# The feed-forward of a transformer block with its weights as the stationary operand of each matmul

## The chip, the cores and the metric

One core of a Trainium2 chip runs the whole program. The metric is the device time of one execution in microseconds; of the kernel before, three runs took 2580.87, 2583.21 and 2591.02 us. One core has a matmul engine (TensorE, PE in the profile, with a lane of its own for weight loads, PEld), VectorE (DVE), ScalarE (ACT), GpSimd (POOL) and SyncE (SP); POOL and SP here mostly issue transfers (DMA).

## What is computed

One layer on 512 tokens of width 2048, all in float32: an input projection, a state-space branch and a differential attention branch, their merge, an output projection, and a gated feed-forward network. Only the last part changes:

```python
x = x + m @ w_out[l]
h = rms_norm(x, norm2_w[l], RMS_EPS)
x = x + (jax.nn.silu(h @ w_ffn_gate[l]) * (h @ w_ffn_up[l])) @ w_ffn_down[l]
```

`rms_norm` divides each token by the root of its mean square and multiplies by a weight per column. The feed-forward width is 5632. The output is x, and the program hands it over transposed, as 2048 columns of the model by 512 tokens (`out` is (D, T); the host turns it round after the run, as it did before).

## The kernel before

**Numbers.** Every large product splits both operands into a high part (float32r, `hi`) and the rest (`lo`), and adds three matmuls: high by high, high by low, low by high. For weights ScalarE copies `raw` into `whi`, and VectorE subtracts into `wlo` (`split`, lines 529 and 530).

**Seven products instead of eight.** The feed-forward cuts each product of matrices into 2 x 2 blocks and computes seven block products (a Winograd form), numbered 1 to 7 in the code. For gate and up, the blocks of x are halves of the tokens (256 each) by halves of the model width (1024 each), and the blocks of the weights are halves of the width by gate and up. For down, they are halves of the tokens by halves of the inner width, and the two column halves of a 1024-column part of `w_ffn_down`. Sums of x blocks are formed once per operand; sums of weight blocks are formed on VectorE as they stream in, in the slab `A` and in `raw` buffers, or by an adding transfer of POOL's queue (line 1316).

**Staging.** The inner width of 5632 is cut into 11 units of 512. For each unit, `ffn` calls `seven` (line 1043) with n = 8 blocks of 128 along the width: each of the seven products is streamed in four chunks of weights, a chunk being 256 rows by 512 columns. `seven` asks `weights(i, c)` for the chunk, splits it, issues its matmuls, and after the last chunk of product i calls `done(i, banks)`, which empties the accumulators into the pieces of the result. Between chunks it pops closures from `fill`. The products of a unit run in the order 1, 2, 7, 5, (6, 3), 4, where (6, 3) means that the chunks of 6 and 3 alternate. Products 6, 3 and 4 go on accumulating in the banks of 1, 5 and 7.

After the 11 units, down runs in six blocks of units ([0], [1, 2], ..., [9, 10]), each for two halves v of the model's columns: 22 unit-halves of seven products with one chunk per unit. Results accumulate in SBUF under the names "11", "5", "7", "x", "53" and "74", after the products in them, and the last block combines them.

**Form A.** A matmul holds a 128 x 128 stationary operand and streams the other one through. Here the stationary one is a tile of 128 tokens (`xh`, `xl`), and the moving one 512 columns of weights: a chunk has 2 blocks x 2 token tiles x 3 = 12 matmuls of 128x512. The results lie with tokens on the partitions. The next stage wants them the other way round, so `flips` (line 1217) transposes 128x128 pieces through TensorE into PSUM banks T and O; in the units, `flip_act` copies them back on ScalarE (line 1254), and `make` forms the seven operands for down from them, which go to memory (`opd`, line 1270) and come back in the down blocks. At the end `final` transposes the finished blocks, adds the residual x2, which lies in memory, and stores.

**Roots.** The reciprocal root of a token's mean square is a value per token. With tokens on the partitions it is a column of scalars (`self.r2`), which ScalarE takes as the scale of its SiLU (line 1333 and 1351) and VectorE as the scalar of a fused multiply (lines 1347 and 1352).

**Order.** TensorE's order is the program's (`manual_schedule`). On the other engines a planner orders the instructions by priority; within an engine they run in the order planned. PSUM has eight banks: four `lin`, two `S`, `T`, `O`. In form A products 1 and 7 take `lin`, 2 and 5 take `S`, the transposes `T` and `O`.

## Time and profile before

| | us |
|---|---|
| median of three runs | 2583.21 |
| the profiled execution | 2578.66 |
| its span, first to last instruction | 2576.9 |
| TensorE busy | 2515.5 |
| VectorE busy | 1912.4 |
| ScalarE busy | 1149.3 |
| first matmul of the feed-forward | 1248 |
| last matmul of the feed-forward ends | 2568.7 |

A row of the groups reads: line, engine, operation, output<-inputs, shapes, count | busy us, mean ns of one | idle time of the engine just ahead of it and what ended it. The time of a matmul in a row is from its start to its end; the next starts before that end, so the pace is read from starts. A chronological row reads: start us, us, engine, line, operation, output<-inputs, shapes, count of like instructions merged. A row of stretches gives busy time and count of each engine in a stretch, the TensorE clock that was granted (1.00 is full), the share of the transfer engines, and GB/s.

### The profile page before, as it was taken

The numbers are of one execution on the slowest core, as the hardware profiler recorded it, in microseconds if no ns is written. First come the engines' busy times: TensorE is split into PE (matmuls) and PEld (weight loads), VectorE is DVE, ScalarE is ACT, GpSimd is POOL, SyncE is SP. The second block draws the span as 40 slices with busy tenths as digits, with TensorE's granted clock in tenths as the row PEclk, the third lists the DMA queues.
The fourth block names the chain that finished last, engine by engine and source line by source line (L and its number), as shares of the span: only waits on it lengthen the run. The fifth ranks groups of instructions, "written<-read, shape, count | busy, mean of one in ns | idle before, by whom it ended". The sixth has DMA issues, their size and how long they took to land.

```text
span 2576.9 us, 32218 instructions
## 1 busy us (share of the span) xinstructions
PE 2515.5 (98%) x11655; PEld 2051.2 (80%) x11655; DVE 1912.4 (74%) x3024; ACT 1149.3 (45%) x1544; POOL 317.4 (12%) x491
## 2 busy tenths in 40 slices
PE   8999999999999999999999999999999998999999
PEld 7788888777777778888788787888888887888887
DVE  7876664777678875535778787788877787788788
ACT  4123332654455543224555554555555555333332
POOL 1012221100010110000001111111101111000000
PEclk9999999999999999999999999999999999999999
DMA  6544554866753434433667666667667697667774
GB/s 190 159 131 124 143 145 132 301 223 221 243 196 104 142 111 156 157 110 129 229 165 219 203 197 208 200 205 236 188 201 208 200 289 289 208 208 236 247 230 150
DMA packets 256400, 491.85 MB, mean 191 GB/s; under 512 B 43448, under 2 KB 43768, under 8 KB 256240
## 3 DMA queue, kind: packets, MB, share of 16 engines
q1 hardware_dynamic: 194160, 352.50, 41.9%
q0 software_dynamic: 49504, 133.04, 18.6%
q10 hardware_dynamic: 12576, 4.24, 0.8%
q8 instruction: 92, 1.51, 0.2%
q14 instruction: 68, 0.56, 0.1%
HBM read 420.35 MB, written 71.96 MB: 191 GB/s over the span
## 4 chain that ended last, share of the span: by engine, by line
PE 50%; issue 30%; DMA 7%; DVE 7%; POOL 4%; ACT 1%; ACTq 0%; SPq 0%; POOLq 0%; DVEq 0%
PE lin L521 24%; PE lin L1068 12%; PE S L1068 8%; DMA raw<-in_w_in_dram 3%; DVE wlo L530 3%; POOL opd L1270 2%; POOL s L1316 1%; DVE raw L1082 1%; DMA raw<-in_w_ffn_up_dram 1%; DVE s L1232 1%; PE S L714 1%; ACT whi L529 1%; DMA s<-in_w_ffn_up_dram 1%; PE S L472 1%; PE O L744 1%
## 5 line engine op out<-in xcount | busy, mean ns | idle before, releaser
L1068 PE MATMUL lin<-whi,s 128*128 128x512 f32 x2400 | 767.4, 393 | 3.3 <-DVE wk L839 2.4
L521 PE MATMUL lin<-s,whi 128*128 128x512 f32 x2432 | 747.6, 397 | 12.5 <-ACT s L535 7.1
L529 ACT ACTIVATE whi<-s 128x1024 fp32r<-128x1024 f32 x351 | 371.0, 1060 | 426.5 <-PE lin L1068 198.8
L521 PEld LDWEIGHTS lin<-s,whi 128*128 128x128 f32 x2432 | 452.8, 189 | 121.5 <-issue 14.1
L1068 PE MATMUL S<-whi,s 128*128 128x512 f32 x1680 | 544.0, 392 | 2.9 <-DVE wk L1232 2.0
L1068 PEld LDWEIGHTS lin<-whi,s 128*128 128x128 f32 x2400 | 453.9, 189 | 99.1 <-issue 2.7
L530 DVE TENSOR_TENSOR wlo<-s,whi 128x1024 fp32r<-128x1024 f32 x351 | 427.7, 1222 | 132.0 <-ACT whi L529 127.6
L1068 PE MATMUL lin<-wlo,s 128*128 128x512 f32 x1200 | 473.2, 394 | 19.9 <-DVE wlo L530 19.9
L521 PE MATMUL lin<-s,wlo 128*128 128x512 f32 x1216 | 455.1, 393 | 0.0
L1068 PEld LDWEIGHTS S<-whi,s 128*128 128x128 f32 x1680 | 315.4, 188 | 68.3 <-ACT whi L529 3.7
L500 DVE TENSOR_TENSOR wlo<-raw,whi 128x1024 fp32r<-128x1024 f32 (+1 forms) x153 | 185.9, 1215 | 218.3 <-ACT whi L499 211.7
L1068 PE MATMUL S<-wlo,s 128*128 128x512 f32 x840 | 328.0, 391 | 6.5 <-DVE wlo L530 6.5
L499 ACT ACTIVATE whi<-raw 128x1024 fp32r<-128x1024 f32 (+1 forms) x153 | 161.0, 1053 | 364.0 <-PE lin L521 324.2
L529 ACT ACTIVATE whi<-raw 128x1024 fp32r<-128x1024 f32 x190 | 199.6, 1057 | 234.5 <-DVE raw L1082 88.0
L1068 PEld LDWEIGHTS lin<-wlo,s 128*128 128x128 f32 x1200 | 227.1, 189 | 77.6 <-DVE wlo L530 31.4
L530 DVE TENSOR_TENSOR wlo<-raw,whi 128x1024 fp32r<-128x1024 f32 x190 | 230.2, 1221 | 56.1 <-ACT whi L529 55.6
L521 PEld LDWEIGHTS lin<-s,wlo 128*128 128x128 f32 x1216 | 229.4, 189 | 48.4
L1068 PEld LDWEIGHTS S<-wlo,s 128*128 128x128 f32 x840 | 157.8, 188 | 42.2 <-DVE wlo L530 10.5
L1270 POOL DMA_DIRECT2D opd<-wk x154 | 90.2, 593 | 679.0 <-ACT wk L529 610.8
L1232 DVE TENSOR_TENSOR s<-s,raw 128x1024 f32<-128x1024 f32 x79 | 96.4, 1222 | 8.9 <-DMA raw<-in_w_ffn_up_dram 7.1
L1082 DVE TENSOR_TENSOR raw<-raw,raw 128x1024 f32<-128x1024 f32 x48 | 58.6, 1224 | 35.4 <-DMA raw<-in_w_in_dram 34.6
L530 DVE TENSOR_TENSOR wk<-s,wk 128x512 fp32r<-128x512 f32 x77 | 52.8, 686 | 39.8 <-DMA opd<-wk 32.2
(409 smaller groups left out, 2330.9 us busy)
## 6 DMA issues: line engine op xcount, KB each, us to landing
raw<-in_w_in_dram SPq DMA_DIRECT2D x175, 512.0 KB, 4.3
raw<-in_w_ffn_up_dram SPq DMA_DIRECT2D x83, 512.0 KB, 4.6
opd<-wk POOLq DMA_DIRECT2D x154, 256.0 KB, 3.8
s<-opd SPq DMA_DIRECT2D x77, 512.0 KB, 9.2
s<-in_w_ffn_down_dram SPq DMA_DIRECT2D x65, 512.0 KB, 6.4
s<-in_w_ffn_gate_dram SPq DMA_DIRECT2D x60, 512.0 KB, 5.1
s<-in_w_ffn_up_dram SPq DMA_DIRECT2D x48, 512.0 KB, 4.2
s<-in_w_ffn_gate_dram POOLq DMA_DIRECT2D x44, 512.0 KB, 7.5
```

The lines of the kernel that those rows point to most:

```text
L472: state = lambda ri, **kw: nc.tensor.matmul(y[:, q * P:(q + 1) * P], w2[:, ri, q].rearrange("p k c -> p (k c)"), sd[:, ri, q].rearrange("p ...
L499: nc.scalar.activation(hi[:, ks], raw[:, ks], AF.Copy)
L500: nc.vector.tensor_tensor(lo[:, ks], raw[:, ks], hi[:, ks].bitcast(F32), op=ALU.subtract)
L521: nc.tensor.matmul(acc[b], l, r, start=(k == 0 and i == 0), stop=(k == nk - 1 and i == 2))
L529: ins = self.nc.scalar.activation(hi, x, AF.Copy)
L530: self.nc.vector.tensor_tensor(lo, x, hi.bitcast(F32), op=ALU.subtract)
L714: nc.tensor.matmul(sp[m], qT[ms, h, i * P:(i + 1) * P], kT[ms, h, 0:W], start=True, stop=True)
L744: nc.tensor.matmul(op[:, h * P:(h + 1) * P], pT[:, kt * P:(kt + 1) * P], v[:, kt, (4 * half + h) * P:(4 * half + h + 1) * P], start=(kt == ...
L1068: nc.tensor.matmul(banks[i][tt], l, r[:, kk, :], skip_group_check=True, start=(i in own and k == 0 and q == 0), stop=(k == n - 1 and q == 2))
L1082: add = lambda o, x, y, op=ALU.add: tt(o, x, y, op=op)
L1232: add = lambda eng, o, x, y, op=ALU.add: eng.tensor_tensor(o, x, y, op=op)
L1270: pool.dma_start(opd[u, i - 1, :, h], hl[h].bitcast(F32))
```

## The change

`seven` gets a `form` argument. In form B, which both feed-forward stages now use, a 128 x 128 tile of weights is stationary and 256 tokens are moving: a chunk has 4 column tiles x 2 blocks x 3 = 24 matmuls of 128x256, two column tiles sharing a bank. The results lie with inner or model columns on the partitions, as the next stage and the output want them. `flips`, `flip_act` and their copies are gone.

A token is now a column, so the roots are needed as a row: `row` multiplies the identity by the scalars and sums it with ones on TensorE, once (`R2`). VectorE multiplies the gate by this row ahead of the SiLU (`silu`), and the finished blocks at the end; the scalar of the fused multiplies is gone. SiLU and its products are put into a list `later`, from which a closure is run ahead of a later chunk's weights.

In the units the order becomes 1, (2, 7), 5, (6, 3), 4, and product 5 takes the banks T and O. In down, "5" and "7" become one accumulator "57"; in the last block some sums of weights are made by adding transfers. `final` multiplies by the row, has x2 added by a transfer (POOL's queue) and stores, up to two stores behind; one piece ("74" of the last half) is finished in `done` of the last product.

On TensorE, at the first chunk of product 2 of a unit in the middle of gate and up. Names: S, O and lin are PSUM banks, whi and wlo the parts of a chunk's weights, s the operand slabs of x, fw and row the results to be transposed; a number tells one buffer from another, and x2 stands for two like instructions in a row. Before, the end of that chunk, four transposes, and the next chunk of product 2:

```order
L1068 MATMUL S_12430<-whi_12433,s_1730_10245 128x512
L1068 MATMUL S_12430<-wlo_12434,s_1730_10245 128x512
L1068 MATMUL S_12430<-whi_12433,s_1730_10245 128x512
L1222 MATMUL O_12449<-ident,fw_12275 128x128
L1222 MATMUL O_12449<-ident,fw_12278 128x128
L1222 MATMUL O_12449<-ident,row_12091 128x128
L1222 MATMUL O_12449<-ident,fw_12094 128x128
L1068 MATMUL S_12429<-whi_12457,s_1730_10245 128x512
L1068 MATMUL S_12429<-wlo_12458,s_1730_10245 128x512
```

Now the end of that chunk, and the first chunk of product 7 behind it:

```order
L1075 MATMUL S_15295<-s_1730_10245,whi_15299 128x256 x2
L1075 MATMUL S_15295<-s_1730_10245,wlo_15300 128x256
L1075 MATMUL S_15295<-s_1730_10245,whi_15299 128x256 x2
L1075 MATMUL S_15295<-s_1730_10245,wlo_15300 128x256
L1075 MATMUL lin_15296<-s_1694_9962,whi_15332 128x256 x2
L1075 MATMUL lin_15296<-s_1694_9962,wlo_15333 128x256
L1075 MATMUL lin_15296<-s_1694_9962,whi_15332 128x256 x2
L1075 MATMUL lin_15296<-s_1694_9962,wlo_15333 128x256
```

The transposes no longer stand between the chunks, the matmuls are half as wide and twice as many, and the chunks of 2 and 7 take turns.

On VectorE, at the end of a unit: lin is the end of product 4, which the two operations with lin add up; wlo_13601 and, now, wlo_15234 are the splits of the third chunk of the next unit's product 1. Before:

```order
L1232 TENSOR_TENSOR c_2247_13461<-c_2247_13461,lin_13133 128x512
L1232 TENSOR_TENSOR s_2248_13464<-s_2248_13464,lin_13134 128x512
L530 TENSOR_TENSOR wlo_13601<-s_1814_10830,whi_13600 128x1024
L1352 SCALAR_TENSOR_TENSOR row_13298<-row_13298,rs_10624,c_2247_13461 128x512
L1352 SCALAR_TENSOR_TENSOR fw_13301<-fw_13301,rs_10624,s_2248_13464 128x512
L530 TENSOR_TENSOR wlo_13618<-s_1814_10830,whi_13617 128x1024
L530 TENSOR_TENSOR wlo_13641<-s_1847_11045,whi_13640 128x1024
L530 TENSOR_TENSOR wlo_13664<-s_1847_11045,whi_13663 128x1024
```

Now:

```order
L1239 TENSOR_TENSOR c_2229_15010<-c_2229_15010,lin_14378 128x512
L1239 TENSOR_TENSOR s_1814_10972<-s_1814_10972,raw_15390 128x1024
L1239 TENSOR_TENSOR s_2230_15013<-s_2230_15013,lin_14379 128x512
L1239 TENSOR_TENSOR c_2229_15010<-c_2229_15010,row_11142 128x512
L530 TENSOR_TENSOR wlo_15234<-s_1814_10972,whi_15233 128x1024
L1239 TENSOR_TENSOR s_2230_15013<-s_2230_15013,row_11142 128x512
L530 TENSOR_TENSOR wlo_15263<-s_1814_10972,whi_15262 128x1024
L1239 TENSOR_TENSOR fw_14763<-fw_14763,c_2229_15010 128x512
L1239 TENSOR_TENSOR fw_14766<-fw_14766,s_2230_15013 128x512
L530 TENSOR_TENSOR wlo_15300<-s_1853_11338,whi_15299 128x1024
```

Ahead of that split stood the two additions; now they have a sum of weights (raw_15390) between them and a multiply by the row (row_11142) behind, and the products with fw, plain now, stand two splits after the additions.

The diff, cut to what matters:

```diff
-    def seven(self, n, weights, ops, done, order=ORDER, fill=(), own=OWN):
+    def seven(self, n, weights, ops, done, order=ORDER, fill=(), own=OWN, form="A"):
...
+                    if form == "B":
+                        for b, kk in ((b, kk) for b in range(4) for kk in range(2)):
+                            k = c + kk
+                            xh, xl = (ops[i][:, h, k, :] for h in range(2))
+                            to = banks[i][b // 2][:, b % 2 * 256:b % 2 * 256 + 256]
+                            for q, (l, r) in enumerate(((hi, xh), (hi, xl), (lo, xh))):
+                                nc.tensor.matmul(to, l[:, kk, b * P:(b + 1) * P], r, skip_group_check=True,
+                                                 start=(i in own and k == 0 and q == 0 and b % 2 == 0),
+                                                 stop=(k == n - 1 and q == 2))
+                    for kk in range(2 if form == "A" else 0):
...
-        tp = self.flips([act[u, tt][:, j * P:(j + 1) * P] for tt in range(4)])
-            nc.scalar.activation(self.E[:, 4 + j], tp, AF.Copy)
...
+        cols = lambda v: v.rearrange("p (c t) -> p c t", c=2)
+        half = lambda th: self.R2[:, 256 * th:256 * th + 256].unsqueeze(1).broadcast_to([P, 2, 256])
+        later = []
+        def silu(x, th):
+            add(dve, cols(x), cols(x), half(th), ALU.mult)
+            nc.scalar.activation(x, x, AF.Silu)
...
+                if c and later and not (first and i == 5):
+                    later.pop(0)()
...
                     elif i == 2:
                         g = st["g", tt] = st["x", tt]
                         add(dve, g, g, p)
-                        nc.scalar.activation(g, g, AF.Silu, scale=r(0))
+                        later.append(lambda g=g: silu(g, 0))
...
                     elif i == 3:
-                        o = act[u, tt] = self.fw()
+                        o = act[u, tt] = self.E[:, 4 + 2 * (u % 2) + tt]
                         add(dve, o, p, st["x", tt], ALU.subtract)
-                        dve.scalar_tensor_tensor(o, o, r(0), st["g", tt], op0=ALU.mult, op1=ALU.mult)
+                        add(dve, o, o, st["g", tt], ALU.mult)
                     elif i == 4:
                         x, d = st["x", tt], st["d", tt]
                         add(dve, x, x, p)
-                        nc.scalar.activation(x, x, AF.Silu, scale=r(1))
-                        dve.scalar_tensor_tensor(d, d, r(1), x, op0=ALU.mult, op1=ALU.mult)
+                        later.append(lambda x=x, d=d: (silu(x, 1), add(dve, d, d, x, ALU.mult)))
...
-            order = (1, 7, 2, 5, (6, 3), 4) if first else self.ORDER
-            self.seven(8, weights, ops, done, order, flips_act(u - 1) + [lambda: None] * 5 + make(u - 1) if u else ())
+            order = (1, 7, 2, 5, (6, 3), 4) if first else (1, (2, 7), 5, (6, 3), 4)
+            self.seven(8, weights, ops, done, order, [lambda: None] * 9 + make(u - 1) if u else (), own={**self.OWN, 5: ("T", "O")}, form="B")
...
+        def final(v, m, th, tt):
+            t, ts = 8 * v + 4 * m + 2 * tt, slice(256 * th, 256 * th + 256)
+            o = cols(acc[v][names[m, th]][:, tt])
+            add(dve, o, o, half(th), ALU.mult)
+            if (v, m, th) == (1, 0, 1):
+                add(dve, o, o, st["x2"][:, 2 * tt:2 * tt + 2])
+                return
+            pool.dma_start(o, rows(x2f, t)[:, :, ts], accum_op=ALU.add)
+            stores.append((rows(out, t)[:, :, ts], o))
+            while len(stores) > 2:
+                pool.dma_start(*stores.pop(0))
...
+                        if last and v and i == 4:
+                            z = self.work()
+                            add(dve, cols(z), cols(p), half(1), ALU.mult)
+                            add(dve, z, z, o)
+                            nc.sync.dma_start(rows(out, 8 + 2 * tt)[:, :, 256:512], cols(z))
...
+                    fill = [f for m in range(2) for th in range(2) for f in both(finals(0, m, th))]
+                    fill += both(finals(1, 0, 0)) + [lambda: None] * 3
+                    fill += both(finals(1, 0, 1)) + both(finals(1, 1, 1)) + both(finals(1, 1, 0))
+                self.seven(n, weights, ops, done, (1, 2, 7, 5, 6, 3, 4), fill, form="B")
...
+        for s in stores:
+            pool.dma_start(*s)
```

97 lines of the change are left out of this document (39 added, 58 removed).

## The prediction

> **What bounds the kernel now.** I read the stretches first: busy time of each engine, the feed-forward part cut into four pieces and the end, and ahead of them a long stretch of the input projection that waits for nothing.
>
> ```profile
> core 0: us, PE busy (x) PEld busy (x) DVE busy (x) ACT busy (x) POOL busy (x), PEclk, DMA share, GB/s
> 1248.00:1300.00 52.00, 46.00 (x195) 36.24 (x194) 47.61 (x69) 30.75 (x42) 1.79 (x5) 0.97 0.81 277
> 1300.00:2100.00 800.00, 793.85 (x3562) 652.79 (x3561) 631.64 (x654) 413.28 (x494) 127.02 (x178) 1.00 0.70 207
> 2100.00:2200.00 100.00, 92.29 (x399) 73.84 (x398) 77.12 (x83) 54.83 (x74) 15.01 (x23) 0.98 0.81 271
> 2200.00:2568.70 368.70, 364.76 (x1621) 299.55 (x1620) 310.39 (x341) 136.37 (x129) 21.58 (x18) 1.00 0.70 216
> 2568.70:2576.90 8.20, 3.43 (x25) 2.35 (x23) 4.54 (x8) 0.00 (x0) 0.00 (x0) 0.93 0.52 193
> 995.00:1195.00 200.00, 200.00 (x884) 165.60 (x884) 93.01 (x116) 65.08 (x82) 10.28 (x19) 1.00 0.43 144
> ```
>
> From 1248 to 2568.7 us, 1320.7 us, TensorE idles 6.0 + 6.2 + 7.7 + 3.9 = 24 us; VectorE is busy 79 to 84% in the long pieces, the transfer engines 70%. So TensorE sets the time, and the first question is its pace. Busy time does not show that, since matmuls overlap; starts do. In the chronological view of TensorE, every third matmul of a dense stretch takes the low part of a chunk:
>
> ```profile
> 1799.89 0.39 PE L1068 MATMUL lin<-wlo,s 128*128 128x512 f32 x1
> ...
> 1805.33 0.39 PE L1068 MATMUL lin<-wlo,s 128*128 128x512 f32 x1
> ```
>
> Between these two lie 24 matmuls (eight triples): 5.44 us / 24 = 226.7 ns each. The feed-forward has 11 units x 7 products x 4 chunks = 308 chunks for gate and up and 11 x 2 x 7 = 154 for down, 462 chunks of 12 matmuls: 5544 x 0.2267 = 1257 us, nearly all of the 1320.7.
>
> **The change, part by part.**
>
> *1. Twice the matmuls, half as wide.* A chunk becomes 24 matmuls of 256 moving columns. The trace has none of that shape, and everything hangs on its pace, so I bound it. Per chunk now: 12 x 226.7 = 2720 ns. Break-even per matmul is 113.3 ns.
>
> The floor is the weight load, which comes twice as often. In one place of the scan part small plain matmuls (64 and 128 columns, four of each in turn) each take fresh 128x128 weights; the lane of weight loads shows:
>
> ```profile
> 195.70 0.53 PEld L472 LDWEIGHTS S<-sd,w 128*128 128x128 f32 x4
> ...
> 198.38 0.30 PEld L472 LDWEIGHTS S<-sd,w 128*128 128x128 f32 x2
> ...
> 181.53 0.19 PEld L521 LDWEIGHTS lin<-s,whi 128*128 128x128 f32 x1
> 181.64 0.19 PEld L521 LDWEIGHTS lin<-s,wlo 128*128 128x128 f32 x1
> ```
>
> Between the first two rows lie six groups of four: 2.68 us / 24 = 111.7 ns for each load with its matmul. Two loads of the kind used here (the other two rows) start 0.11 apart, as fast. A load runs beside the matmul before it. So 24 x 111.7 = 2681 ns: 0.039 us a chunk less, x 462 = -18 us at best.
>
> The ceiling comes from the clock. At half clock (granted 0.50) the same wide matmul and a transpose run at:
>
> ```profile
> 814.40:821.20 6.80, 5.73 (x18) 4.86 (x19) 6.23 (x26) 3.18 (x7) 0.77 (x1) 0.50 0.16 62
> ...
> 818.09 0.63 PE L521 MATMUL lin<-s,wlo 128*128 128x512 f32 x1
> 820.65 0.63 PE L521 MATMUL lin<-s,wlo 128*128 128x512 f32 x1
> ...
> 816.16 0.42 PE L693 MATMUL S<-ident,aw 128*128 128x128 f32 x1
> 816.38 0.42 PE L744 MATMUL O<-s,aw 128*128 128x128 f32 x1
> ```
>
> Six wide matmuls in 2.56 us, 426.7 ns each; at full clock half of that would be 213.3, and the trace has 226.7. So 13.3 ns is added at full clock. If it is an add-on for each instruction, 256 columns take 106.7 + 13.3 = 120 ns: 2880 a chunk, +0.160 x 462 = +74 us. If it grows with the columns, 256 take 113.3, and the chunk costs the same. The transposes speak for the second:
>
> ```profile
> 1351.24 0.27 PE L1222 MATMUL T<-ident,row 128*128 128x128 f32 x1
> 1351.35 0.27 PE L1222 MATMUL T<-ident,fw 128*128 128x128 f32 x1
> ```
>
> They take 0.21 to 0.22 us at half clock and 0.11 at full, so an instruction of this kind has no add-on of 13 ns, and the plain matmuls above, also 128 columns in half of them, go at 111.7 with their loads. But they are other kinds. I take 114 ns, between the load's 111.7 and 120 but next to the reading by columns: 24 x 114 = 2736, +0.016 x 462 = **+7 us**, ends -18 and +74.
>
> The Trainium skill, TensorE: Matmul & The Clock Gate, section Back-to-back issue gap, gives a warm gap of columns / 2.4 plus a fixed 2.5 ns, so 215.8 and 109.2 ns for 512 and 256; the 226.7 here disagrees with the first. By that rule the chunk would go from 2590 to 2621 ns, an estimate of +14 us: an add-on per instruction speaks against splitting, only with a smaller add-on than the 13.3 of this trace.
>
> *2. The transposes go.* Rows by form of the transposing line (the T twin of each has the same count):
>
> ```profile
> L1222 PE MATMUL O<-ident,fw 128*128 128x128 f32 x66 | 13.2, 272 | 0.0
> L1222 PE MATMUL O<-ident,row 128*128 128x128 f32 x22 | 6.0, 272 | 0.0
> L1222 PE MATMUL O<-ident,s 128*128 128x128 f32 x32 | 5.2, 279 | 1.0 <-DVE s L1232 1.0
> ```
>
> 2 x (66 + 22) = 176 in the gate/up units and the start of down, and of the 64 at the end 48 stand ahead of the last big matmul (12 groups of four; the other 16 are in the tail). 224 x 0.109 = **-24 us**, all on TensorE's path. The copies on ScalarE that emptied them go too; ScalarE is half idle (413 of 800), so that is worth nothing more.
>
> *3. Roots as a row.* A root per token was a scalar per partition, free inside the SiLU and the product; now the gate gets a multiply of its own, 4 per unit, 44 in all, at the price of a 128x512 VectorE operation, against a fused one that becomes plain. VectorE's groups by form between 1300 and 2100 us (splits and sums of weights first):
>
> ```profile
> L530 DVE TENSOR_TENSOR wlo<-s,whi 128x1024 fp32r<-128x1024 f32 x208 | 253.3, 1222 | 63.5 <-ACT whi L529 59.6 <-DMA s<-in_w_ffn_gate_dram 3.2
> L1232 DVE TENSOR_TENSOR s<-s,raw 128x1024 f32<-128x1024 f32 x49 | 59.9, 1222 | 7.5 <-DMA raw<-in_w_ffn_up_dram 6.9
> ...
> L1347 DVE SCALAR_TENSOR_TENSOR fw<-fw,rs,wk 128x512 f32<-128x512 f32 x20 | 14.9, 744 | 0.0
> L1232 DVE TENSOR_TENSOR wk<-wk,S 128x512 f32<-128x512 f32 x20 | 13.1, 680 | 0.0
> ```
>
> 44 x 0.68 = 30 us, less 44 x 0.06 = 3. VectorE has 168 us idle in those 800, and the added 27 us take it from 79% to some 82%: hidden, **0**. Without that cover they would cost their 27 us. What waits there now is the split of the next weights, which is queued on VectorE behind the unit's last products. Waits between 1260 and 2100 us, in total, times and longest:
>
> ```profile
> PEld lin L1068 <- DVE wlo L530: 14.8, 15, 2.7
> PE lin L1068 <- DVE wlo L530: 9.0, 9, 2.4
> ```
>
> The two overlap, being two lanes of one engine. Does the order now make a split late? At a unit's end the split of the next unit's third chunk stands behind two additions and one multiply (0.68 each) and one or two long sums of weights (1.22 each), with 1.22 of its own: 4.5 to 5.7 us from the moment product 4 is done. The two chunks ahead of it, split already, give TensorE 5.4 us from that moment, and the low part is asked for 0.2 later. So it comes just in time; before, with two additions only (2.6 us), the margin was 3 us. This is the spot where a new wait would show.
>
> *4. Products 2 and 7 alternate, 5 on other banks.* Product 7 asks three 128x1024 operations of VectorE per chunk (two sums, one split), product 2 one, each of about 1.22 us. Four chunks of 7 in a row ask 14.6 us of VectorE against 10.9 of TensorE; a pair of chunks asks 4.9 against 5.4. Together with part 3 I give the boundaries **-4 us** of the 24 idle, ends -10 and +10. Product 5 accumulates in the two banks that the transposes leave, and no longer waits for product 2's to be emptied; this is in the same number. The down part keeps its order, and its stalls.
>
> *5. The tail.* Now:
>
> ```profile
> 2568.35 0.39 PE L1068 MATMUL lin<-whi,s 128*128 128x512 f32 x1
> ...
> 2572.86 0.68 DVE L1232 TENSOR_TENSOR s<-s,T 128x512 f32<-128x512 f32 x1
> ```
>
> and transfers, size and us to landing (the second from the last 477 us):
>
> ```profile
> opd<-wk POOLq DMA_DIRECT2D x154, 256.0 KB, 3.8
> ...
> out_dram<-s SPq DMA_DIRECT2D x8, 256.0 KB, 2.1
> ```
>
> From the last matmul's end, 2568.74, to 2576.9 are 8.2 us: transposes and additions in turn, then stores. Afterwards the last 53 and 57 blocks get their residual from an adding transfer on POOL's queue, and their stores are queued on POOL behind it, so each waits for that one to land. VectorE still has about two of the six short operations ahead of it when TensorE ends (1.2 us); the adding transfer of 256 KB takes 3.8 us or more, the store 2.1 to 3.8, and three such pairs go one behind the other's issue: some 8 to 11 us. On SP, beside it, five more operations (3.1 us) and a store (2.1) are earlier. **+2 us**, ends 0 and +4.
>
> *Sum:* 7 - 24 + 0 - 4 + 2 = -19 us against the profiled execution, whose span is 2576.9 and whose time is 2578.66, so 2559.7. The median of the three runs shown is 2583.21, 4.6 above it; for such a median I forecast 2564 us.
>
> **The rivals.**
>
> A. *A fixed add-on of 13.3 ns for each matmul*: +74 - 24 - 4 + 2 = +48, 2631 us, slower. It decides from 114 + 19 / (462 x 24) x 1000 = 115.7 ns per narrow matmul on. For it: 226.7 against 213.3 is all that is known of this type. Against it: transposes and plain matmuls show no such add-on. Any other loss of pace with twice the instructions (a load that doesn't quite hide, since 111.7 against 113.3 leaves no room) ends on this side too; at 125 ns it would be 2631 + 55 = 2686.
>
> B. *VectorE takes the gain*: its 27 us are not hidden, because they fall at the unit ends, where the split comes just in time. 2564 + 10 to 27 = 2574 to 2591, no change. For it: waits for the low part are the largest that TensorE has; against it: 21% idle, and (2, 7) evens the load.
>
> C. *The load is the bound and the add-on vanishes*: 111.7 ns, -18 for +7: 2539 us. The change then does more than drop transposes.
>
> D. *The change doesn't drop the transposes' time*, because TensorE would have waited there anyway. But their rows show 1.0 us of idle time or none ahead of them; I give it nothing.
>
> **How the numbers follow.** Forecast 0.55, with a range of its own from 2547 to 2581 (a ns of pace is 11 us, parts 4 and 5 some 6 more); A with its kin 0.27; B 0.10; C 0.08. The range for 8 in 10: from 2537, just under C, to 2631, A. Half a percent, about what a measurement tells here, is 13 us: faster is below 2570, slower above 2596. Of the forecast 0.45 lies below 2570 and 0.10 between; with C 0.53 faster. Same: 0.10 + 0.08 of B + 0.01 of A = 0.19. Slower 0.28.
>
> **What would show it.** In the changed profile, starts of the narrow matmuls in a dense stretch: 113 to 115 ns apart (forecast), 120 (A), 112 (C). TensorE's idle time between 1300 and 2100 some 2 to 6 us, no waits for the low part longer than 2 us; if those grow to 20 us and more, B. No transposing line after 1250 us. From the last matmul to the end 8 to 12 us, ending in stores of POOL's queue. The forecast is wrong if the pace is above 115.7 ns, whatever the rest does.

## The result and the profile after

The changed kernel takes 2619.95 us (median of 4 runs, 2617.35 to 2621.87), the kernel before beside it 2586.58 (2580.87 to 2591.02): a ratio of 1.013 with an interval of 1.0103 to 1.0156, so 27 to 40 us slower. The prediction had the other sign. In the two profiled executions the span grows from 2576.9 to 2620.1 us, 43.2, a little above that interval: the profiled execution of the kernel before, 2578.66 us, is faster than the four behind its median, that of the changed kernel the slowest of its four.

First the stretches of the changed kernel, with the columns of the prediction's first view: the feed-forward part now ends at 2606.6 us, and the last row is the tail behind it.

```profile
1248.00:1300.00 52.00, 47.72 (x370) 46.79 (x370) 47.06 (x72) 28.87 (x39) 2.17 (x4) 0.93 0.82 283
1300.00:2100.00 800.00, 800.00 (x6667) 799.80 (x6667) 636.89 (x680) 381.44 (x443) 120.69 (x167) 1.00 0.68 202
2100.00:2200.00 100.00, 97.87 (x812) 97.26 (x811) 83.68 (x94) 56.04 (x74) 18.19 (x28) 1.00 0.76 247
2200.00:2570.00 370.00, 368.43 (x3066) 367.82 (x3065) 301.98 (x328) 135.75 (x130) 40.16 (x37) 1.00 0.74 226
2570.00:2606.60 36.60, 27.51 (x205) 26.84 (x203) 20.35 (x28) 6.25 (x6) 12.91 (x13) 0.86 0.69 138
2606.60:2620.10 13.50, 0.04 (x1) 0.00 (x0) 3.36 (x6) 0.00 (x0) 5.34 (x6) 0.60 0.68 161
```

In the 800 us of the units TensorE doesn't idle at all (before: 6.15 us), and it starts 6667 matmuls there: 800 / 6667 = 120.0 ns each. That is the pace of rival A. The one large wait is in the last row but one, at 2577 us; in order of time on TensorE:

```profile
2571.56 0.28 PE L1075 MATMUL S<-s,wlo 128*128 128x256 f32 x1
...
2576.96 0.28 PE L1075 MATMUL S<-s,wlo 128*128 128x256 f32 x1
2585.88 0.80 PE L1075 MATMUL lin<-s,whi 128*128 128x256 f32 x2 [8.63 <-ACT whi L529]
...
2588.58 0.41 PE L1075 MATMUL lin<-s,wlo 128*128 128x256 f32 x1
...
2591.78 0.41 PE L1075 MATMUL lin<-s,wlo 128*128 128x256 f32 x1
```

Between the first two rows lie 15 triples: 5.40 us / 45 = 120.0 ns again. Then 8.63 us of idle time pass until the next weights are split. The matmuls behind that start at half clock (granted 0.50 from 2588 to 2592 us): between the last two rows lie five triples, 3.20 us / 15 = 0.213 us each. Up to 2594 us the starts fall 12.1 us behind a pace of 120 ns; that is what this place costs. What is late is seen on POOL, whose queue carries the adding transfers of weights (L1440 and L1449), those of x2 (L1389) and stores (L1393, L1490):

```profile
2571.85 0.76 POOL L1393 DMA_DIRECT2D out_dram<-s  x1 [4.45 <-DMA s<-x2d]
2573.21 0.73 POOL L1393 DMA_DIRECT2D out_dram<-s  x1 [0.60 <-DMA s<-x2d]
2573.93 2.54 POOL L1389 DMA_DIRECT2D s<-x2d  x2
2575.45 2.25 POOL L1440 DMA_DIRECT2D s<-in_w_ffn_down_dram  x1
...
2606.06 3.65 POOL L1389 DMA_DIRECT2D s<-x2d  x3 [0.52 <-DVE s L1239]
2610.80 0.76 POOL L1393 DMA_DIRECT2D out_dram<-s  x1 [1.10 <-DMA s<-x2d]
2612.26 0.75 POOL L1490 DMA_DIRECT2D out_dram<-s  x1 [0.70 <-DMA s<-x2d]
2614.79 0.72 POOL L1490 DMA_DIRECT2D out_dram<-s  x1 [1.78 <-DMA s<-x2d]
```

The matmuls that wait are those of product 6, which follows product 5 here. The transfer that makes the sum of its weights (L1440) is issued only at 2575.45, behind two stores that waited 4.45 and 0.60 us for x2 to land and two further x2 transfers; and the transfer itself then takes 9.2 us, as the chain that ended last has it:

```profile
2575.45 9.21 DMA s<-in_w_ffn_down_dram
```

The queue is not all of it. VectorE's split of product 5's first chunk, which reads the same slab, ends at 2568.8, so the queue held this transfer for up to 6.7 us. Issued at 2568.8 and with the same 9.2 us to landing, it would still have come at 2578.0, and ScalarE needs 1.06 us more for the high part, where TensorE was out of work at 2577.2: an estimate of some 2 us of wait without any queue.

The last four rows of POOL are the tail: three x2 transfers, then three stores, each waiting for a landing. From the start of the last matmul to the end are 13.7 us, before 8.5.

**Where the time went.** Counted from the starts of all matmuls from the first to the last of the part (1320.4 us before, 1357.2 after):

| | before | after | difference |
|---|---|---|---|
| matmuls at their pace (5543 x 226.7, 11087 x 120.0 ns) | 1256.6 | 1330.4 | +73.8 |
| 216 transposes and 8 small matmuls before, 16 small ones after (110 ns) | 24.6 | 1.8 | -22.8 |
| the rest: waits and half clock | 39.2 | 25.0 | -14.2 |
| the part | 1320.4 | 1357.2 | +36.8 |

With a start that is 1.3 us later and a tail longer by 5.2 this is the 43.2. Of the 25.0 after, 12.1 are the place at 2577 us. So three questions: what sets 120 ns, why 26 us of other waits went away, and what the last block's queue costs.

### The profile page after: what moved, and what is told of

The parts are those of the page before. It is cut to its first block, busy times and chain, and to the rows that moved or that the text cites. A ratio compares the mean times of both kernels' runs of the same rounds, so it can differ in the third digit from the quotient of the medians.

```text
span 2620.1 us, 43011 instructions
## 1 busy us (share of the span) xinstructions
PE 2554.0 (97%) x16967; PEld 2321.6 (89%) x16967; DVE 1933.3 (74%) x3073; ACT 1121.1 (43%) x1496; POOL 350.2 (13%) x523
## 4 chain that ended last, share of the span: by engine, by line
PE 59%; issue 21%; DMA 7%; DVE 7%; POOL 3%; ACT 1%; ACTq 0%; SPq 0%; POOLq 0%; DVEq 0%
PE lin L521 29%; PE lin L1075 14%; PE S L1075 5%; DMA raw<-in_w_in_dram 4%; PE O L1075 3%; PE T L1075 3%; DVE wlo L530 3%; POOL opd L1280 2%; DMA s<-in_w_ffn_down_dram 1%; DVE raw L1097 1%; DVE s L1239 1%; ACT whi L529 1%; PE S L714 1%; PE O L744 1%; PE S L472 1%
## 5 line engine op out<-in xcount | busy, mean ns | idle before, releaser
L1075 PE MATMUL lin<-s,whi 128*128 128x256 f32 x4224 | 770.6, 284 | 10.1 <-ACT whi L529 10.1
L1075 PEld LDWEIGHTS lin<-s,whi 128*128 128x128 f32 x4224 | 662.6, 193 | 10.4 <-ACT whi L529 10.4
L1075 PE MATMUL lin<-s,wlo 128*128 128x256 f32 x2112 | 600.7, 284 | 6.2 <-DVE wlo L530 6.2
L521 PEld LDWEIGHTS lin<-s,whi 128*128 128x128 f32 x2432 | 452.7, 189 | 122.0 <-issue 14.7
L1075 PEld LDWEIGHTS lin<-s,wlo 128*128 128x128 f32 x2112 | 407.5, 193 | 7.8 <-DVE wlo L530 7.7
L1075 PE MATMUL S<-s,whi 128*128 128x256 f32 x1760 | 320.2, 283 | 0.0
L1075 PEld LDWEIGHTS S<-s,whi 128*128 128x128 f32 x1760 | 274.5, 192 | 0.0
L521 PEld LDWEIGHTS lin<-s,wlo 128*128 128x128 f32 x1216 | 229.4, 189 | 48.5
L1075 PE MATMUL S<-s,wlo 128*128 128x256 f32 x880 | 249.2, 283 | 0.6 <-DVE wlo L530 0.6
L1075 PEld LDWEIGHTS S<-s,wlo 128*128 128x128 f32 x880 | 168.9, 192 | 1.0 <-DVE wlo L530 1.0
L1075 PE MATMUL T<-s,whi 128*128 128x256 f32 x704 | 130.6, 283 | 0.0
L1075 PE MATMUL O<-s,whi 128*128 128x256 f32 x704 | 130.5, 283 | 0.0
L1075 PEld LDWEIGHTS O<-s,whi 128*128 128x128 f32 x704 | 109.8, 192 | 0.0
```

The source lines that it names most:

```text
L521: nc.tensor.matmul(acc[b], l, r, start=(k == 0 and i == 0), stop=(k == nk - 1 and i == 2))
L1075: nc.tensor.matmul(to, l[:, kk, b * P:(b + 1) * P], r, skip_group_check=True, start=(i in own and k == 0 and q == 0 and b % 2 == 0), stop= ...
```

## The experiments

### The pace: the old form with narrow matmuls

```diff
-    nc.tensor.matmul(banks[i][tt], l, r[:, kk, :], ...)
+    for e in range(2):
+        es = slice(256 * e, 256 * e + 256)
+        nc.tensor.matmul(banks[i][tt][:, es], l, r[:, kk, es], ...)
```

> The kernel before, with each matmul of the feed-forward part that moves 512 columns written as two of 256 on the same weights; nothing else is changed, so transposes, roots and order stay. Theory one, a fixed add-on for each matmul: 11088 matmuls at 120.0 ns in place of 5544 at 226.7, +74 us, some 2660 us beside a kernel before of 2586. Theory two, the 120 ns of the changed kernel belong to its own form (fresh weights as the stationary operand, activations moving) and not to the width: two halves at 113.3 ns cost what the wide one did, 0 us. Theory three, a weight load that doesn't quite hide: between the two, from 111.7 ns (-18 us) to 120 ns.

Measured: 2638.14 us, ratio 1.0215 (1.0201 to 1.0229), +56 us. The units' stretch:

```profile
1300.00:2100.00 800.00, 799.74 (x6674) 798.97 (x6673) 606.14 (x623) 397.05 (x473) 119.27 (x166) 1.00 0.67 194
```

Of the 6674 starts in 800 us 148 are transposes (16 a unit, 0.11 us each); the others take 783.7 / 6526 = 120 ns, in the old form too. So the pace belongs to the width, not to the form, and theory two falls. But the time grew by 56 and not by 74: the 6 us of idle time of this stretch are 0.26 here, and the waits and half clock of the whole part fell from 39 to some 22 us. At 2880 ns a chunk in place of 2720 VectorE has more time for each one.

### The add-on by width and by operand

Two kernels carry twelve and eleven rows of 24 test matmuls in the dense stretch of a unit. "Rounded" is the type of the products here (float32r), "plain" is float32; the profile writes f32 for both. For example:

```diff
+    for j in range(24):
+        mm(to[:, 0:384], xs[j % 8], hi[:, 0, 0:384], start=j == 0, stop=j == 23)
```

> The kernel before, with twelve rows of 24 test matmuls behind the second chunk of product 7 in the fifth unit, into a bank that nothing reads for the output: the rounded type moving 512, 384, 320, 256, 192 and 128 columns with fresh weights each time; 256 columns on one and the same weights; 256 columns on weights of 64 and of 32 columns; the plain type moving 128 and 64; and 512 once more. Fixed add-on: 226.7, 173.3, 146.7, 120.0 ns, then 111.7 and 111.7 where the load takes over, and 120 on the same and on narrower weights too. An add-on by the columns: 226.7, 170, 141.7, 113.3. A load of 120 ns that is the bound of the narrow ones: 226.7, 173 or 170, 142 to 147, then 120, 120, 120, and less than 120 at 256 columns where the weights have only 64 or 32 columns.

Start and length of each row of 24 (the last two are the plain type, which runs as two passes, x48; the twelfth row, 512 columns once more, takes 227 ns between most starts):

```profile
1362.39 5.60 PE L1050 MATMUL T<-whi,s 128*128 128x512 f32 x24
1367.83 4.35 PE L1052 MATMUL T<-whi,s 128*128 128x384 f32 x24
1372.01 3.67 PE L1054 MATMUL T<-whi,s 128*128 128x320 f32 x24
1375.53 3.04 PE L1056 MATMUL T<-whi,s 128*128 128x256 f32 x24
1378.40 2.82 PE L1058 MATMUL T<-whi,s 128*128 128x192 f32 x24
1381.06 2.81 PE L1060 MATMUL T<-whi,s 128*128 128x128 f32 x24
1383.71 3.09 PE L1062 MATMUL T<-whi,s 128*128 128x256 f32 x24
1386.64 2.89 PE L1064 MATMUL T<-whi,s 128*64 128x256 f32 x24
1389.37 2.88 PE L1066 MATMUL T<-whi,s 128*32 128x256 f32 x24
1392.09 5.52 PE L1068 MATMUL T<-whi,s 128*128 128x128 f32 x48
1397.45 5.47 PE L1070 MATMUL T<-whi,s 128*128 128x64 f32 x48
```

From one row's start to the next, over the count: 226.7, 174, 146.7, 119.6 ns for 512, 384, 320 and 256 columns. At half clock (granted 0.50) 512 columns took 426.7 ns in the kernel before, so at full clock 0.417 ns a column; less that, 13.3, 14, 13.3 and 13 ns are left: a fixed add-on. At 192 and 128 columns the rounded type takes 110.8 and 110.4, at 128 and 64 the plain one 111.7 and 109.8 a pass: a floor that doesn't depend on the moving columns. I put it down to the weight load, since it is gone with 16-bit weights (55.8 ns at 128 columns, below). The same weights each time change nothing (120 between starts, with one gap of 170). One miss: weights of 64 or 32 columns take 113.8 and 113.3 ns, half the add-on, where 120 was expected.

```diff
+        for j in range(24):
+            mm(to[0:96, 0:256], xs[j % 8][:, 0:96], hi[:, 0, 0:256], ...)
...
+        for j in range(24):
+            mm(to[:, 0:256], bs[j % 4], bx[:, 0:256], ...)    # bx: 16 bits
```

> The kernel before, with eleven rows of 24 test matmuls at the same place as in the first such kernel. Known from that: 13.3 ns over the columns at 2.4 GHz with weights of 128 columns, 6.7 with 64 or 32. Now: the rounded type moving 256 columns with the two banks in turn, with weights of 96 columns, moving 512 with weights of 64 columns, 256 with 64 rows of weights and of moving data; the plain type moving 256; 16-bit operands moving 512, 256 and 128. If the add-on is the swap of the weights: 96 columns lie between 6.7 and 13.3, 512 columns on narrow weights take 220.0, half the rows change nothing or halve it, and 16-bit weights, half as many bytes, show less than 13.3. If it belongs to the moving data or to the bank: 13.3 with narrow weights at 512 columns, less with two banks or half the rows.

```profile
1366.54 3.04 PE L1056 MATMUL T<-whi,s 128*128 128x256 f32 x24
1369.41 0.28 PE L1058 MATMUL T<-whi,s 128*128 128x256 f32 x1
...
1372.29 2.94 PE L1060 MATMUL T<-whi,s 128*96 128x256 f32 x24
1375.07 5.68 PE L1062 MATMUL T<-whi,s 128*64 128x512 f32 x24
1380.68 3.13 PE L1064 MATMUL T<-whi,s 64*128 64x256 f32 x24
1383.74 10.63 PE L1066 MATMUL T<-whi,s 128*128 128x256 f32 x48
1394.42 5.13 PE L1068 MATMUL T<-wk 128*128 128x512 bf16 x23
1399.39 2.78 PE L1070 MATMUL T<-wk 128*128 128x256 bf16 x24
1402.01 1.50 PE L1072 MATMUL T<-wk 128*128 128x128 bf16 x24
```

Two banks in turn (the row at 1369.41 and those left out) take 120.0 ns, so does half the rows between most starts: neither bank nor rows matter. Weights of 96 columns take 116 ns, between the two, but 512 columns on 64-column weights take some 230, not 220, so that the weights' width is no clean explanation. What separates the rows clearly is the operands' type: 16-bit operands take 215.8 and 109.2 ns for 512 and 256 columns between most starts, an add-on of 2.5 (of the first row's 24 one has no record). And the plain type takes 216 ns for each pass of 256 columns, as long as 16-bit ones take for 512: half the speed by column, with an add-on of about 2.7. The Trainium skill, TensorE: Matmul & The Clock Gate, section Back-to-back issue gap, has columns / 2.4 plus 2.5 ns; the 16-bit rows agree with it, the rounded type with its 13.3 does not. What in the rounded type makes the 13.3 stays open. The length of a weight load is one rival: in the load lane's records of these two kernels it falls from 192 ns at 128 weight columns to 161, 134 and 108 at 96, 64 and 32, as the add-on does; but the loads of the plain type take 190 ns too, beside an add-on of 2.7.

### The transposes' price, and what takes half of it back

In the kernel before, the copies read the untransposed tiles:

```diff
-            tp = self.flips([act[u, tt][:, j * P:(j + 1) * P] for tt in range(4)])
-            nc.scalar.activation(self.E[:, 4 + j], tp, AF.Copy)
+            nc.scalar.activation(self.E[:, 4 + j], act[u, j], AF.Copy)
...
-            tp = self.flips(parts)
+            tp = self.flips(parts) if (v, m) == (1, 0) else acc[v][(...)[m][j // 2]][:, j % 2]
```

> The kernel before with 224 of its 240 transposes left out (the output is then not the product: the copies read the untransposed tiles instead); the 16 behind the last matmul stay, so that the tail keeps its form. Theory one, the transposes stand on TensorE's path: 224 x 0.109 = -24 us. Theory two, TensorE would have waited there anyway, or the stalls at product 7 grow by what it gains, since VectorE's sums and splits are then late: -5 to -15 us.

Measured: 2568.86 us, ratio 0.995 (0.9936 to 0.9963), -13 us: theory two. The stretch of the units, and what TensorE waited for in it (total, times, longest), first here and then in the kernel before:

```profile
1300.00:2100.00 800.00, 781.87 (x3420) 639.76 (x3419) 633.07 (x657) 417.97 (x497) 128.92 (x181) 1.00 0.70 210
```

```profile
PE lin L1068 <- DVE wlo L530: 16.2, 14, 1.8
PE lin L1068 <- DVE wlo L530: 5.8, 6, 1.8
```

TensorE idles 18 us of the 800 instead of 6, at product 7 of each unit. The 24 us are gone from its path, and longer waits take up 11 of them by the time; most of these are for VectorE's split. To see what VectorE waits for there, four more kernels, first with the sum for product 5 moved from VectorE to POOL's queue:

```diff
-                        add(dve, A, A, r1)
+                        pool.dma_start(A, two(b(1, 2)), accum_op=ALU.add)
```

> The kernel before without 224 transposes (the copies read the untransposed tiles, so the output is not the product) and with that same sum on POOL's queue. Without the transposes alone the kernel gained some 13 us of the 24, and its stalls at product 7 grew to 1.7 to 1.9 us a unit. Theory one, VectorE at product 7 took the rest: with the sum gone from it, -24 to -30 us against the kernel before. Theory two, something else took it: -10 to -16 us still.

Measured: 2579.94 us, 0.9978 (0.9964 to 0.9992), so worse than without the move; neither theory. In the same stretch VectorE is busy 580 us, no longer 633, but the transfers' share went from 0.70 to 0.83, and VectorE's wait for a load of product 7 grew from 15.5 to 37.6 us:

```profile
1300.00:2100.00 800.00, 773.06 (x3379) 632.20 (x3379) 580.10 (x610) 413.22 (x489) 172.74 (x214) 1.00 0.83 232
```

```profile
DVE raw L1232 <- DMA raw<-in_w_ffn_up_dram: 37.6, 14, 4.8
```

So the experiment changed two things. The next pair changes one each, still without transposes; first one load a chunk at product 7 with all of VectorE's operations, then all loads and one sum fewer:

```diff
-                    r1, r2 = load(raw(), b(1, 2)), load(raw(), b(2, 2))
-                    add(dve, r2, r1, r2)
+                    r1, r2 = load(raw(), b(1, 2)), raw()
+                    add(dve, r2, r1, r1)
```

> The kernel before without 224 transposes, and with one load for each chunk of product 7 in the units instead of two (the sum adds the first to itself; neither the transposes nor w22's part of the sum is computed). VectorE's operations are all there; 44 transfers of 512 KB are left out. Theory one, the stalls at product 7 are loads that land late, since 1 MB a chunk waits for free buffers: they go, and the kernel is 23 to 28 us below the kernel before, not 13. Theory two, VectorE's three operations are the bound: -13 us, as with two loads.

```diff
-                    if not first:
-                        add(dve, A, A, r1)
```

> The kernel before without 224 transposes, and without product 7's second sum (A + w12) in all units but the first; all loads are there, and 40 VectorE operations of 1.22 us are left out (their part of product 5's and later products' weights is then missing). Theory one, late loads: -13 us still, or a few more. Theory two, VectorE is the bound: -23 to -28 us. If both kernels of this pair gain, either one alone would have been enough to let the other catch up.

Measured: 2561.5 us, 0.9925 (0.9908 to 0.9942), -19 us, and 2556.63 us, 0.9908 (0.9894 to 0.9921), -24 us. The units' stretch of the one and of the other:

```profile
1300.00:2100.00 800.00, 790.44 (x3469) 649.52 (x3468) 639.67 (x665) 427.02 (x506) 131.81 (x184) 1.00 0.63 186
```

```profile
1300.00:2100.00 800.00, 791.22 (x3475) 650.79 (x3474) 597.09 (x628) 426.92 (x506) 131.94 (x184) 1.00 0.70 212
```

TensorE's idle time falls from 18 us to 9.6 and 8.8. Of the missing 11 us the one load fewer regains 6, the one sum fewer all: late loads and three operations a chunk add up on VectorE, and taking either away lets it catch up, in full or for the larger part. The transposes were cover for that. No run leaves out the load or the sum with the transposes in place, so what either would be worth there isn't shown.

Last, both at once in the old form: narrow matmuls and no transposes.

```diff
+            nc.scalar.activation(self.E[:, 4 + j], act[u, j], AF.Copy)
...
+        nc.tensor.matmul(banks[i][tt][:, es], l, r[:, kk, es], ...)
```

> The kernel before without 224 transposes (again not the product) and with every wide matmul of the feed-forward part as two of 256 columns: the pace of the changed kernel and the transposes away, in the old form. The split alone cost some 56 us, since 15 of its 74 were taken out of stalls. Theory one, at 120 ns a matmul VectorE keeps up, and the transposes now count in full: 56 - 24 = +32 us. Theory two, the stalls at product 7 come back by what the transposes leave, as in the kernel without them: +40 to +45 us.

Measured: 2624.04 us, 1.0157 (1.0134 to 1.0179), +41 us: theory two, and some 14 us less than with the transposes. The wait for the low part is back: in the 800 us 6.8 us in 8 times, with the transposes 0.2 us in one. So in this order even at 120 ns a matmul VectorE is late once the transposes are gone.

### Products 2 and 7 in turn

In the changed kernel, the old order:

```diff
-            order = (1, 7, 2, 5, (6, 3), 4) if first else (1, (2, 7), 5, (6, 3), 4)
+            order = (1, 7, 2, 5, (6, 3), 4) if first else self.ORDER
```

> The changed kernel with products 1, 2, 7, 5 one after the other again in all units but the first (product 5 stays in its two banks). Theory one, the alternation keeps VectorE from falling behind at product 7: +5 to +12 us, with waits for the low part of 0.5 to 2 us in each unit. Theory two, at 120 ns a matmul VectorE has 2880 ns a chunk and is not late in either order: 0 to +1 us and no such waits.

Measured: 2629.89 us, ratio to the kernel before 1.0188 (1.0173 to 1.0204), where the changed kernel has 1.013: +10 to +15 us, theory one, at the upper end of its range or above it. The wait that the alternation had removed:

```profile
PE lin L1075 <- DVE wlo L530: 8.4, 8, 1.7
```

And in the kernel before, the new order, at 227 ns:

```diff
-            order = (1, 7, 2, 5, (6, 3), 4) if first else self.ORDER
+            order = (1, 7, 2, 5, (6, 3), 4) if first else (1, (2, 7), 5, (6, 3), 4)
...
+                       own={**self.OWN, 5: ("T", "O")})
```

> The kernel before, with products 2 and 7 alternating in all units but the first and product 5 in the two banks that the transposes leave; the form, the transposes and the roots stay. Theory one, the stalls at product 7 go because the two weight sums of product 7 are spread over twice the time: -5 to -12 us, about -8. Theory two, the stalls went in the changed kernel because its TensorE is slower (2880 against 2720 ns a chunk) and VectorE has more time for each chunk: 0 to -3 us at the old pace.

Measured: 2580.96 us, 0.9999 (0.999 to 1.0007): nothing. Here the wait only moved, from product 7 (lin, 5.8 us in the kernel before, 1.0 here) to product 5's banks:

```profile
PE T L1068 <- DVE wlo L530: 6.1, 10, 1.9
```

Setting product 2's additions behind the splits there did not help either.

```diff
-                        add(dve, g, g, p)
-                        nc.scalar.activation(g, g, AF.Silu, scale=r(0))
+                        later.append(lambda g=g, p=p, s=r(0): (add(dve, g, g, p), nc.scalar.activation(...)))
```

> The kernel before with products 2 and 7 alternating, product 5 in the other two banks, and the two additions and SiLUs of product 2 queued behind the splits of product 5's second chunk. Alternating alone left a stall of 0.4 to 1.0 us at product 5's first chunk in each unit, in place of the one at product 7. Theory one, that stall is product 2's additions, which stand on VectorE ahead of the split that product 5 waits for: it goes, -5 to -8 us. Theory two, VectorE is behind by the whole of the sums and the stall only moves on once more: 0 us.

Measured: 2582.18 us, 0.9995 (0.9984 to 1.0006). Theory two: the stall at product 5 stays (4.2 us in 10 waits). So the same order is worth 10 us or more at 2880 ns a chunk and without transposes, and nothing at 2720 with them; no run separates the two conditions.

### The root multiplies

```diff
-            add(dve, cols(x), cols(x), half(th), ALU.mult)
             nc.scalar.activation(x, x, AF.Silu)
```

> The changed kernel without the 44 multiplies by the root row ahead of SiLU (the gate's argument then lacks the root; the multiplies at the end stay). Theory one, VectorE's 30 us for them are hidden: 0 us, within 1. Theory two, they delay the splits at the units' ends: -5 to -27 us.

Measured: 2617.9 us, 1.0139 (1.0123 to 1.0154) against 1.013: no difference. VectorE's busy time in the 800 us falls by 27 us, TensorE's stays full:

```profile
1300.00:2100.00 800.00, 799.52 (x6659) 798.94 (x6658) 610.31 (x638) 383.18 (x442) 119.50 (x168) 1.00 0.70 203
```

### The last block and the tail

```diff
-                        if last and v:
-                            pool.dma_start(A, two(blk(1, 2)), accum_op=ALU.add)
-                        else:
-                            add(dve, A, A, r)
+                        add(dve, A, A, r)
...
-                    if i == 6 and last and v:
-                        pool.dma_start(A, two(blk(2, 2)), accum_op=ALU.add)
-                    elif i == 6:
+                    if i == 6:
```

> The changed kernel, with the weight sums of products 7 and 6 in the very last block made by VectorE as before, not by adding transfers on POOL's queue. Theory one, the 8.6 us wait at 2577 us is those transfers queued on POOL behind the output's adding transfers and stores: -9 to -12 us with the half clock behind it, some 2608 us. Theory two, the wait is for something else that is late there (the second sum of product 4, still on POOL, or VectorE's own load from the finished blocks): 0 to -3 us.

Measured: 2615.08 us, 1.0122 (1.0107 to 1.0138), some 5 us below the changed kernel by the medians, though the two intervals overlap. In the trace the wait is gone, as theory one had it: the feed-forward part is 11.2 us shorter (1346.0), and TensorE waits between 2550 and 2600 us only for this:

```profile
PE lin L1075 <- DVE wlo L530: 1.3, 2, 0.8
```

That those transfers are the cause is shown; the run takes them away altogether, so it doesn't part the queue ahead of them from their own 9.2 us. But the tail grew from 13.7 to 17.5 us, since the same row of x2 transfers and stores on POOL now lies behind the last matmul. Next, that row too:

```diff
-                pool.dma_start(*stores.pop(0))
+                (nc.sync if v else pool).dma_start(*stores.pop(0))
...
-            pool.dma_start(*s)
+            nc.sync.dma_start(*s)
```

> The changed kernel with VectorE's weight sums in the last block, and the stores of the last half of the output on SyncE's queue, so that no adding transfer of x2 is queued behind a store that waits for the one before it to land. Theory one, the tail is that row on POOL's queue: 17.5 us from the last matmul's start to the end become 12 to 13, -4 to -5 us beside the kernel with the sums alone, some 2610 us. Theory two, each adding transfer's own landing and the store's set the end: 0 to -2 us.

Measured: 2606.26 us, 1.0093 (1.0079 to 1.0107), 9 us below the last by the medians and 7 by the ratios, more than either theory gave. The tail is 12.4 us, 5.1 less, as theory one had it; the rest stands ahead of it in the trace (the part is 1.3 us shorter and starts 3.5 us earlier, which this edit doesn't reach). The x2 transfers on POOL follow one another without a store between them:

```profile
2590.49 1.20 POOL L1389 DMA_DIRECT2D s<-x2d  x1 [2.10 <-DVE s L1239]
2592.53 2.44 POOL L1389 DMA_DIRECT2D s<-x2d  x2 [0.84 <-DVE s L1239]
```

Of the changed kernel's loss, then, 10 us by the ratios (1.30 and 0.93%) to 14 us by the medians came of what the change put on POOL's queue; 24 us remain (0.93% of 2583.5).

### A kernel that beats both

The trace of before shows stalls of TensorE between 2165 and 2180 us. ScalarE's loads of x2 for the end of the kernel stand there, early, ahead of its copies. The profile names a load of `opd` as what ended the idle time there; that the x2 loads cause it is shown by the last run of this section:

```profile
2166.21 0.33 ACTq L1373 DMA_DIRECT2D wk<-x2d  x1
2166.59 1.09 ACT L1437 ACTIVATE s<-lin 128x512 f32<-128x512 f32 x2 [4.87 <-DMA s<-opd]
...
2173.89 0.33 ACTq L1373 DMA_DIRECT2D wk<-x2d  x1
2174.26 1.09 ACT L1437 ACTIVATE s<-lin 128x512 f32<-128x512 f32 x2 [3.72 <-DMA s<-opd]
```

Two easings of the kernel before, first together:

```diff
-                nc.scalar.dma_start(o, x2d[t])
+                self.behind(nc.scalar.dma_start(o, x2d[t]))
...
-            ... flips_act(u - 1) + [lambda: None] * 5 + make(u - 1) if u else ()
+            ... flips_act(u - 1) + [lambda: None] * 5 + apart(make(u - 1)) if u else ()
```

> The kernel before in its old order, with two of its queues eased: the eight loads of x2 that ScalarE issues for the first half of the output stay behind the last block's splits (five of them now stand on ScalarE between 2152 and 2174 us, hold work buffers and wait there up to 4.9 us), and the seven steps that make the down operands of a unit are set one slot apart, from product 5 to product 4, instead of one after the other. Theory one, ScalarE and VectorE are late for the splits because of what is queued ahead of them: the stalls between 2150 and 2177 us and half of those at product 7 go, -4 to -10 us. Theory two, product 7's own three operations a chunk are all that matters: only the 3 us of the first part.

Measured: 2575.96 us, 0.9974 (0.9962 to 0.9987). With the alternation and the later additions besides:

```diff
+            order = (1, 7, 2, 5, (6, 3), 4) if first else (1, (2, 7), 5, (6, 3), 4)
...
+                        later.append(lambda g=g, p=p, s=r(0): (add(dve, g, g, p), nc.scalar.activation(...)))
```

> The same two easings, with products 2 and 7 alternating, product 5 in the other banks and product 2's additions later. Theory one, with the steps apart VectorE is no longer behind when product 5 begins, so that the alternation now pays: -8 to -14 us against the kernel before. Theory two, the alternation is worth nothing at 227 ns a matmul whatever stands beside it: as the kernel with the easings alone.

Measured: 2583.56 us, 1.0004 (0.9994 to 1.0014): the alternation costs what the easings gave, and the wait at product 5 is 16.1 us in 10 times. Neither theory. With product 7's second sum on POOL's queue, as above, but in the eased kernel:

```diff
-                        add(dve, A, A, r1)
+                        pool.dma_start(A, two(b(1, 2)), accum_op=ALU.add)
```

> The eased kernel before, with product 7's second weight sum in each unit but the first (A + w12, needed only at product 5) made by an adding transfer on POOL's queue and no longer by VectorE: 40 operations of 1.22 us fewer there, 40 transfers of 512 KB more. Theory one, the stalls at product 7 are VectorE's three operations a chunk: with two, 2.44 us against 2.72 of TensorE, they go, -5 to -9 us against the eased kernel. Theory two, the transfer takes its own landing (8.8 us for such a transfer in the changed kernel) and is late for product 5, or holds up POOL's other work: 0 to +10 us.

Measured: 2597.73 us, 1.005 (1.0033 to 1.0068), 20 us worse than without, beyond both ranges; the transfers' share is 0.82 here too. Last, the x2 loads alone:

```diff
-                nc.scalar.dma_start(o, x2d[t])
+                self.behind(nc.scalar.dma_start(o, x2d[t]))
```

> The kernel before with only the first of the two easings: the eight loads of x2 stay behind the last block's splits. Theory one, the gain of 6.7 us with both easings came from here: -3 to -7 us, no stalls between 2165 and 2180 us. Theory two, it came from the steps set apart: 0 to -2 us.

Measured: 2575.63 us, 0.9976 (0.9966 to 0.9986): all of the gain, within the noise. ScalarE's waits for `opd` between 2140 and 2200 us, 8.6 us before, are gone. In the changeover from the units to the down part TensorE was busy 92.29 of 100 us before, and now:

```profile
2100.00:2200.00 100.00, 97.09 (x431) 78.82 (x430) 81.51 (x87) 57.08 (x76) 15.70 (x24) 1.00 0.84 275
```

Alone or with the steps set apart, this is the fastest of the kernels here that compute the product, 6 to 7 us below the kernel before.

## Why the prediction was wrong, step by step

**The step that failed is part 1, "I take 114 ns".** It measured 120.0, the upper end, +73.8 and not +7 us. The two ends were worked out correctly and the pace for the change of sign, 115.7, was named; the choice between them was wrong. It rested on transposes and plain matmuls that "show no such add-on". They don't, but they are another type: the plain type runs at half speed by column and its add-on is about 2.7 ns, so that 109 ns for 128 columns says nothing on the rounded type. The prediction's own rows at half clock had a sign of it: 0.22 us for a transpose of 128 columns, where 426.7 ns for 512 of the rounded type are 106.7 for 128. The 226.7 against 213.3 of the same type was the only evidence that counted, and it could not tell an add-on by instruction from one by column. That was a reason for even odds on A, not for 0.27. Rival A was right in its mechanism. Its +48 came out as +43 in the two traces and +33 by the medians: 26 us of waits went, where it took 4 off, and 12 us at 2577 and a longer tail came. That its 2631 lies close to 2620 is in part luck.

**Part 2, the transposes, was right on the path and wrong on the end.** All 24 us left TensorE (216 transposes and not 224: of the 64 at the end 24 stand behind the last wide matmul, not 16, which is 1 us); in the old form the kernel gained 13 of them. The prediction priced the stalls at product 7 and the transposes apart, though the one is cover for the other. Rival D, given nothing, was half true: not that TensorE would have waited there, but that it waits later. Rival B's mechanism, VectorE taking the gain, is close to this one, but at product 7 and not at the units' ends. In the changed kernel the alternation keeps that wait away.

**Part 3, roots as a row at 0, was right**, by the run without them; and the split that "comes just in time" at a unit's end did come in time: no wait for the low part in the 800 us.

**Part 4, -4 us with ends of -10 and +10, was mis-sized.** In the changed kernel the alternation is worth 10 us or more, and all 6 us of idle time between 1300 and 2100 are gone. Over the part 26 us of waits went, where it gave 4; the kernel with narrow matmuls alone loses 17 of its 39, so much of that is the slower pace. The prediction's sum, 4.9 us of VectorE against 5.4 of TensorE, should have given a gain at the old pace too, and there is none. It left out what else stands on VectorE in those chunks; which of it makes product 5 late at the old pace was not settled.

**Part 5, the tail, +2 with ends of 0 and +4, measured +5.2.** The row of x2 transfers and stores on POOL was named, and its price was too low: it took 3.8 us for the landing of an x2 transfer, from plain stores of the same size (`opd`), and 2.1 to 3.8 for an output store on this queue; in the changed kernel the medians are 5.3 and 4.2.

**Not foreseen: 12 us at 2577 us.** The prediction did not count the adding transfers of weights that the change moves onto POOL's queue in the last block, behind the x2 transfers and stores that it puts there as well. Such a transfer then takes 9.2 us to land, where VectorE needs 1.22 us for the sum. Each was visible in the change.

Of the signs that the prediction named, the starts are 120 ns apart, as A had it. The idle time in the 800 us is 0 and not 2 to 6 us, and there is no wait for the low part in them. No transposing line is left. The tail is 13.7 us, above the 8 to 12, and ends in POOL's stores.

## What to carry to other kernels

Before an operand's role is exchanged so that a matmul becomes narrower, price the narrow matmul from rows of the same type; if the trace has one width only, an add-on for each instruction is as likely as any, and a short row of test matmuls in the dense stretch settles it. An engine that is 79% busy can still be the limit of one stage, so that work removed from the busier engine pays only as far as the next stall: count what the other engine owes in that stage before counting the gain. On a queue that works in order, list everything that stands ahead of a transfer that an engine will wait for, and what each of those waits for.

## What the runs showed of the hardware that was not expected

- The rounded type (float32r) has an add-on of 13 to 14 ns for each matmul at full clock, from 256 to 512 columns, whatever the bank, the rows or the reuse of weights; 16-bit operands have 2.5 ns, and the plain type takes 216 ns for a pass of 256 columns. Weights of 64 or 32 columns bring the 13.3 down to 6.7 at 256 columns (113.5 ns), but not at 512 (some 230).
- At half clock the add-on is not there: the changed kernel's matmuls of 256 columns then start 0.213 us apart, 0.833 ns a column, as the 426.7 ns for 512 columns in the kernel before.
- With four-byte weights of 128 columns, narrower matmuls end at a floor of 110 to 112 ns. The Trainium skill, TensorE: Matmul & The Clock Gate, section LDWEIGHTS (loading the stationary operand), has columns / 1.2, so 106.7; the floor here is 3 to 5% above that.
- Forty adding transfers of 512 KB on POOL's queue raised the share of the transfer engines from 0.70 to 0.82 and the loads that share them came later for VectorE (its wait for product 7's loads went from 15.5 to 37.6 us without the transposes). VectorE had 50 to 70 us less to do in the 800, and yet the kernel was 20 us slower with the transposes and 7 to 11 without them.
